# A second wave's input projection moved between the first wave's expert lists, in buffers of its own

## The chip, the cores and the metric

The kernel runs on one NeuronCore of a Trainium2 chip. The metric is the device time of one execution in microseconds; 1798.25 us is the median of three runs before the change (1796.3 to 1800.18).

## The reference

One decoder layer works on 512 prompt tokens and 8 sample tokens, all in f32, model width 1024.

```
x_n   = rmsnorm(x) * g1
proj  = x_n @ w_in                # 3584 columns: attention q,k,v; retention q,k,v; gate
cat   = [dilated attention (8 heads x 64) | gated retention (4 heads x 128)]
h     = x + cat @ w_out
hn    = rmsnorm(h) * g2
q     = hn @ w_pq                 # 8 heads x 2 x 128
top16 of q @ sub_keys, twice; 256 sums of pairs -> top16: 16 expert ids and weights g per head
a     = gelu(sum(u[eid] * hn))    # 8 x 16 experts of 16384, each one row of 1024
y     = h + sum(g * a * v[eid])
out   = rmsnorm(y) * gf
```

The samples attend to a cache of 2048 keys and carry a retention state. Keys, values and states are outputs too.

## The kernel before, in words

The 512 prompt tokens go through in two waves of 256. The 8 samples ride with the first wave up to the end of their mixer, and with the second from its output projection on.

The experts are handled in two ways. The first wave's 256 tokens and the samples *gather*: for each of their 16 experts per head GpSimd issues an indirect DMA that brings one row of `peer_u` to each of 128 partitions (line 907, 128 x 1024 f32), VectorE takes the dot product with the token (line 925), and later does the same with `peer_v` and a weighted sum (line 939). One such fetch with its VectorE work is a *step*: 512 of them for the first wave, 32 for the samples (on 64 partitions). Eight buffers hold rows. The second wave's 256 tokens are *dense*: for each of 128 blocks of 128 experts, `dense_a` multiplies all tokens by a block of `peer_u` (`ut`, line 1054), `dense_w` multiplies by a mask of weights (line 1169), `dense_y` by a block of `peer_v` (`vt`, line 1176). The masks come from `scatter` (lines 1142 to 1157), a chunk of 64 blocks at a time.

In the order of the program: the first wave's input projection, attention and retention, with the samples' attention; its output projection and norm (`outer(0)`, which leaves `hn` in `hnD`); its lists (`product_keys(0)`: projection `w_pq`, scores `psco`, copied to `sc`, top-16 on VectorE at lines 253 to 353); the second wave's load, norm, input projection `in_proj(1)` in 28 blocks of 128 columns, `outer(1)` and `product_keys(1)`, whose result overwrites `hnD`; the scatter of chunk 0; then the dense loop.

The gather steps are one generator, `work`. `beside` runs some steps of it after every block of another generator, by the table `STEPS`; `run` in the scatter loop takes `SOON` steps over 32 groups, and the dense loop takes `RATE - EARLY - SOON` over 128 blocks, where `EARLY` counts the earlier ones. A scheduler of the framework then settles the order of each engine's queue, within the dependencies. Each engine works its queue strictly in order, and so does SyncE, which issues the loads of weights and the stores.

Pools on the right side of the on-chip memory are stacked: a pool opened after another has closed takes over its bytes, and its first writer waits for the last reader there. Thus `x1B`, `xTB` and `catB` of the second wave lie where the lists of the first wave had their temporaries.

Of the kernel before, what the change touches and what calls it, by code (L numbers as in the profile page):

```python
# [34 lines left out]
GBUFS, UTB, VTB, OHB, AHEAD = 8, 4, 4, 2, 19  # L35
ORDER = "aayyyy"
FIRST = 6
SCB = 4
PTB = 2
FOLD = True  # L40
LASTA = False
CHUNKS = [0, 64, 128]
ROWS = max(b - a for a, b in zip(CHUNKS, CHUNKS[1:]))
NG = DT // 8
STEPS = (8, 3, 2, 6)
SOON, RATE = 48, 600
AHEAD0 = 14


# [1 line left out]
def step_kernel(ctx, tc, x_prompt, x_sample, cache_k, cache_v, state_ret, norm1_g, w_in, ret_gn_g,  # L51
# [20 lines left out]
    ps = front.enter_context(tc.tile_pool(name="ps", bufs=2, space=PSUM))  # L72
    wp = front.enter_context(tc.tile_pool(name="wp", bufs=2, side="right"))
    fc = front.enter_context(tc.tile_pool(name="fc", bufs=1, side="right"))
    smp = ExitStack()
    sp = smp.enter_context(tc.tile_pool(name="sp", bufs=1))
    kvp = smp.enter_context(tc.tile_pool(name="kvp", bufs=2))
# [342 lines left out]
    def attention(w, hp2, q2, put):  # L420

        po = ps_tile("o", "po")
        bh = [wide("bh", "bh") for j in range(2)]
        for j in range(2):
            nc.scalar.activation(bh[j], bias, AF.Copy, scale=SLOPES[2 * hp2 + j])
        for t in range(2):
            T = 2 * w + t
            n = (T + 1) * 128
            off = 384 - 128 * T
            pTs = []  # L430
            for j in range(2):
                psc = ps_tile("s", "psc")
                nc.tensor.matmul(psc[:, :n], q2[j][:, t * 128:(t + 1) * 128], keys[hp2][:, :n], start=True, stop=True)
                lg = wide("lg", "lg", 3)[:, :n]
                nm = small.tile([128, 1], F32, name="nm", tag="nm")
                nc.vector.tensor_tensor_reduce(out=lg, in0=psc[:, :n], in1=bh[j][:, off:off + n],
                                               scale=-0.125, scalar=-LOWEST, op0=OP.add, op1=OP.min, accum_out=nm)
                nc.scalar.activation(lg, lg, AF.Exp, bias=nm, scale=-1.0)
                sm = small.tile([128, 1], F32, name="sm", tag="sm")
                nc.vector.tensor_tensor_reduce(out=lg, in0=lg, in1=mult[:, off:off + n],  # L440
                                               scale=1.0, scalar=0.0, op0=OP.mult, op1=OP.add, accum_out=sm)
                rs = small.tile([128, 1], F32, name="rs", tag="rs")
                nc.vector.reciprocal(rs, sm)
                nc.scalar.activation(lg, lg, AF.Copy, scale=rs)
                pT = ps_tile("tr", "pT")
                for s in range(T + 1):
                    nc.tensor.transpose(pT[:, s * 128:(s + 1) * 128], lg[:, s * 128:(s + 1) * 128], ident)
                pTs.append(wide("pTs", "pTs", PTB)[:, :n])
                nc.scalar.activation(pTs[j], pT[:, :n], AF.Copy)
            for s in range(T + 1):  # L450
                for j in range(2):
                    nc.tensor.matmul(po[j * 64:(j + 1) * 64, t * 128:(t + 1) * 128],
                                     vals[hp2][:, s, j * 64:(j + 1) * 64],
                                     pTs[j][:, s * 128:(s + 1) * 128], start=(s == 0), stop=(s == T))
        put(po[:, :WT], hp2)

    def groupnorm(pool, po, p, nb, tag="tr"):
# [5 lines left out]
        for b in range(nb):  # L463
            nc.vector.bn_aggr(mv[:p, b, :], bs[:p, b, :])
        r = rstd_of(mv[:p, :nb, 1], 1.0, 1e-5, p, nb, tag)
        yo = pool.tile([128, 512], F32, name="yo", tag="pTs", bufs=PTB if pool is pools["ap"] else 1)
        for b in range(nb):
            nc.vector.tensor_scalar(yo[:p, b * 128:(b + 1) * 128], po[:p, b * 128:(b + 1) * 128],
                                    mv[:p, b, 0:1], r[:p, b:b + 1], op0=OP.subtract, op1=OP.mult)
# [10 lines left out]
    def retention(w, h, rqT, rkT, kdN, rvN):  # L480
        pin = ps_tile("s", "pin")
        for T in range(2):
            cs = slice(T * 128, (T + 1) * 128)
            nc.tensor.matmul(pin[:, cs], rkT[:, cs], rqT[:, cs], start=True, stop=True)
        inn = wide("lg", "inn", 3)[:, :WT]
        nc.vector.tensor_tensor(out=blk(inn), in0=blk(pin[:, :WT]), in1=dmat[:, h:h + 1, :].to_broadcast([128, 2, 128]),
                                op=OP.mult)
        qd = wide("bh", "qd")[:, :WT]
# [390 lines left out]
    all_of(in_proj(0, xT, [k * 4 + h for h in range(1, 4) for k in range(3, 7)], putA))  # L879
    mixA.close()  # L880

    def outer(w, c2, hn, outs):

        ost = ExitStack()
        op_ = ost.enter_context(tc.tile_pool(name="op", bufs=1, side="right"))
        x = op_.tile([128, 2, D], F32, name="xo")
        xs = op_.tile([8, D], F32, name="xs") if w else None
        load_x(w, x, xs)
        ssq2 = small.tile([128, 3, KB], F32, name="ssq2", tag="ssq2", bufs=1)
        nc.vector.memset(ssq2, 1.0)  # L890
        yield from out_proj(op_, c2, x, xs, ssq2)
        norm2(op_, w, x, xs, ssq2, hn)
        ost.close()
# [54 lines left out]
            w = w2  # L948
        return y, x

    def finish(halves, p, x, dst):

        for q, y in enumerate(halves):
            cs = slice(q * 512, (q + 1) * 512)
            nc.vector.tensor_tensor(out=x[:p, cs], in0=y, in1=x[:p, cs], op=OP.add)
        o = pe.tile([128, D], F32, name="fin", tag="fin")
        ssq = small.tile([128, 1], F32, name="ssqf", tag="ssqf")
        nc.scalar.activation(o[:p], x[:p], AF.Square, accum_out=ssq[:p])
        r = rstd_of(ssq[:p], D, 1e-6, p)
# [17 lines left out]

    def gathered():
        y, x = yield from experts(lists[0], [hnr[:128, :]], slice(0, 128))
        store = finish((y[:, 0:512], y[:, 512:]), 128, x, yp2[0:128, :])  # L980
        y, x = yield from delayed(experts(lists[1], [hnr[128:GT, :]], slice(128, GT)), 12, store)
        store = finish((y[:, 0:512], y[:, 512:]), 128, x, yp2[128:GT, :])
        y64, x = yield from delayed(experts(listS, [hnr[GT:, :]] * 8, slice(512, 520)), 12, store)
        yS = gp.tile([128, D], F32, name="yS", tag="rows")[:8]
        for q in range(2):
            ph = banks["a"]()
            nc.tensor.matmul(ph[:8], selT, y64[:, q * 512:(q + 1) * 512], start=True, stop=True)
            nc.scalar.activation(yS[:, q * 512:(q + 1) * 512], ph[:8], AF.Copy)
        finish((yS[:, 0:512], yS[:, 512:]), 8, x, y_s.rearrange("b t d -> (b t) d"))()

    work = gathered()

# [18 lines left out]
    def run(g, n=1):  # L1011
        for _ in range(n):
            if g is not None:
                next(g, None)

    hst = ExitStack()
    beside(product_keys(0, lists[:2], None, hnA), 8, 0)
    run(work, STEPS[0])
    mixB = ExitStack()
    cpB = mixB.enter_context(tc.tile_pool(name="cpB", bufs=1, side="right"))  # L1020
    catB = cpB.tile([128, KB, WT + 8], F32, name="catB")
    inB = ExitStack()
    xtB = inB.enter_context(tc.tile_pool(name="xtB", bufs=1, side="right"))
    xTB = xtB.tile([128, KB, WT], F32, name="xTB")
    xst = ExitStack()
    xp = xst.enter_context(tc.tile_pool(name="xpB", bufs=1, side="right"))
    x1 = xp.tile([128, 2, D], F32, name="x1B")
    load_x(1, x1)
    norm1(xp, x1, None, lambda pt, k: nc.scalar.activation(xTB[:, k, :], pt, AF.Copy, scale=g1T[:, k:k + 1]))
    xst.close()  # L1030
    pools["ap"] = inB.enter_context(tc.tile_pool(name="apB", bufs=2, side="right"))

    def putB(bank, cb):
        nc.scalar.activation(catB[:, cb, :WT], bank, AF.Copy)

    nc.vector.tensor_copy(catB[:, :, WT:], catS)
    beside(in_proj(1, (xTB,), [k * 4 + hp for hp in range(4) for k in range(3)] +
                   [k * 4 + h for h in range(4) for k in range(3, 7)], putB), 28, STEPS[1])
    inB.close()
    beside(outer(1, (catB,), hnD, None), 8, STEPS[2])  # L1040
    mixB.close()
# [41 lines left out]
        run(first, 2 * (AHEAD0 * (h + 1) // PH - AHEAD0 * h // PH))  # L1083

    beside(product_keys(1, lists[2:], listS, hnD), 8, STEPS[3], early)
    EARLY = step[0] + STEPS[0]
    front.close()

    den = ExitStack()
# [204 lines left out]
```

## Time and profile before

| | |
|---|---|
| median of three runs | 1798.25 us |
| profiled execution: own time, span | 1801.39, 1799.6 us |
| busy in the span: TensorE, VectorE, ScalarE, GpSimd | 1518.8, 1207.2, 420.1, 798.9 us |
| read from memory, over the span | 495.56 MB, 281 GB/s |

All times of rows are microseconds from the start of the span. A matmul of f32 data leaves two records, so a line that the program holds 256 times stands with x512. DVE is VectorE, PE TensorE, POOL GpSimd, SP SyncE.

### The profile page before, as it was taken

The page shows a single profiled execution, that of the slowest core. Times are in us where ns is not written, and L with a number is a line of the kernel's source. Part 1 is how long each engine was busy: PE and PEld are TensorE (multiplying, and loading weights), DVE is VectorE, ACT ScalarE, POOL GpSimd, SP SyncE. Part 2 cuts the span into 40 slices and gives each one's busy share as a digit, 9 for nine tenths or more (in the row PEclk, how much of TensorE's full clock was granted, in tenths as well). Part 3 has the DMA queues.
Part 4 walks back from the last instruction along what each step waited for, and adds up shares of the span by engine and source line. Part 5 has one row for each costly group of instructions (what it writes and reads, how often), then busy time and mean ns, then how long its engine had stood idle before and what let it go on. Part 6 is the DMA issues. An engine that isn't in the chain of part 4 may idle for free.

```text
span 1799.6 us, 21781 instructions
## 1 busy us (share of the span) xinstructions
PE 1518.8 (84%) x7544; PEld 1113.2 (62%) x7544; DVE 1207.2 (67%) x2893; ACT 420.1 (23%) x849; POOL 798.9 (44%) x672
## 2 busy tenths in 40 slices
PE   5977779105898769995469999999999999999997
PEld 5976547104677558884356666666666666666643
DVE  5776517998688643879997775667665555555573
ACT  6734402103532221324331121111111000000001
POOL 2155220287456550005876554444445445455550
PEclk9988889657999879995569999999999999999999
DMA  7576564499899972436759999999999899999995
GB/s 201 154 216 225 185 205 150 130 347 387 280 354 368 366 275 78 158 113 221 228 191 352 400 408 334 340 347 342 347 347 348 340 367 362 370 356 360 309 243 166
DMA packets 213327, 506.89 MB, mean 282 GB/s; under 512 B 16424, under 2 KB 103000, under 8 KB 213088
## 3 DMA queue, kind: packets, MB, share of 16 engines
q0 software_dynamic: 82208, 295.80, 45.9%
q1 hardware_dynamic: 131008, 209.68, 34.6%
q8 instruction: 60, 0.98, 0.2%
q14 instruction: 51, 0.42, 0.1%
HBM read 495.56 MB, written 9.86 MB: 281 GB/s over the span
## 4 chain that ended last, share of the span: by engine, by line
PE 66%; DVE 14%; DMA 10%; issue 2%; ACT 1%; POOL 1%; SPq 0%; DVEq 0%; ACTq 0%; POOLq 0%
PE y L1176 23%; PE pa L1054 21%; PE pa L152 11%; DVE u L925 3%; PE pg L1155 3%; PE paF L1054 3%; DMA raw<-in_w_in 2%; DVE y L939 2%; DVE oi L1149 1%; DMA vt<-in_peer_v 1%; DMA hs<-xo 1%; DMA raw<-in_w_out 1%; DMA pq<-sq_d 1%; DMA u<-in_peer_u,eidL 1%; DVE oj L1144 1%
## 5 line engine op out<-in xcount | busy, mean ns | idle before, releaser
L907 POOL DMA_INDIRECT u<-in_peer_u,eidL x256 | 337.4, 1318 | 321.6 <-DVE a L925 90.3
L1176 PE MATMUL y<-vt,ge 128*128 128x512 f32 x1024 | 462.4, 598 | 3.6 <-DMA vt<-in_peer_v 3.6
L907 POOL DMA_INDIRECT v<-in_peer_v,eidL x256 | 335.0, 1309 | 273.0 <-DVE y L939 115.6
L1054 PE MATMUL pa<-hnD,ut 128*128 128x256 f32 x1792 | 407.7, 381 | 2.5 <-ACT ge L1058 2.0
L1054 PEld LDWEIGHTS pa<-hnD,ut 128*128 128x128 f32 x1792 | 339.5, 191 | 78.2 <-issue 35.1
L939 DVE SCALAR_TENSOR_TENSOR y<-v,gw,y 128x1024 f32<-128x1024 f32 (+1 forms) x269 | 345.1, 1283 | 32.3 <-DMA v<-in_peer_v,eidL 16.4
L925 DVE CUSTOM_DVE_ANT_0 u<-u,hq 128x1024 f32<-128x1024 f32 (+1 forms) x272 | 324.2, 1221 | 18.3 <-DMA u<-in_peer_u,eidL 14.9
L1176 PEld LDWEIGHTS y<-vt,ge 128*128 128x128 f32 x1024 | 196.4, 192 | 207.0 <-issue 194.8
L1169 DVE TENSOR_TENSOR ge<-ge,big 128x256 f32<-128x256 f32 x128 | 51.2, 427 | 187.8 <-ACT ge L1058 179.2
L1058 ACT ACTIVATE ge<-pa 128x256 f32<-128x256 f32 x112 | 42.6, 381 | 475.3 <-PE pa L1054 472.3
L1155 PEld LDWEIGHTS <-oj 128*128 128x128 bf16 x1536 | 101.2, 167 | 83.2 <-DVE oi L1149 62.8
L152 PE MATMUL pa<-hnD,raw 128*128 128x256 f32 (+1 forms) x512 | 122.6, 393 | 0.0
L152 PE MATMUL pa<-xTB,raw 128*128 128x256 f32 x448 | 107.0, 393 | 10.5 <-DMA raw<-in_w_in 10.0
L152 PEld LDWEIGHTS pa<-hnD,raw 128*128 128x128 f32 x512 | 97.8, 196 | 19.9 <-issue 5.9
L1155 PE MATMUL pg<-oi,oj 128*128 128x64 bf16 x1152 | 77.8, 233 | 33.6 <-DVE oi L1149 33.6
L152 PEld LDWEIGHTS pa<-xTB,raw 128*128 128x128 f32 x448 | 86.3, 198 | 25.4 <-issue 7.0
L1144 DVE TENSOR_TENSOR oj<-iota,l 128x1024 bf16<-128x1024 bf16 x64 | 44.2, 692 | 71.0 <-PE pg L1155 71.0
L1157 ACT ACTIVATE big<-pg 128x512 f32<-128x512 f32 x48 | 52.8, 1099 | 152.7 <-PE pg L1155 150.3
L391 PE MATMUL pt<-ident,x1B 128*128 128x128 f32 x16 | 3.6, 388 | 95.2 <-ACT x1B L386 95.2
L121 PE MATMUL pa<-xT,wh 128*128 128x264 f32 x224 | 70.3, 315 | 9.8 <-ACT xT L114 4.8
L253 DVE MAX8 valL<-sc 128x8 f32<-128x128 f32 x64 | 14.3, 280 | 90.6 <-ACT sc L845 76.8
L122 PE MATMUL pa<-xT,wh 128*128 128x264 f32 x224 | 68.2, 305 | 0.1
(515 smaller groups left out, 1852.4 us busy)
## 6 DMA issues: line engine op xcount, KB each, us to landing
ut<-in_u_turned SPq DMA_DIRECT2D x128, 512.0 KB, 6.7
vt<-in_peer_v SPq DMA_DIRECT2D x128, 512.0 KB, 4.4
raw<-in_w_in SPq DMA_DIRECT2D x56, 512.0 KB, 6.6
raw<-in_w_pq SPq DMA_DIRECT2D x16, 1024.0 KB, 5.2
raw<-in_w_out SPq DMA_DIRECT2D x8, 1024.0 KB, 9.8
kv<-in_cache_k_win POOLq DMA_DIRECT2D x24, 256.0 KB, 5.1
kv<-in_cache_v_win POOLq DMA_DIRECT2D x24, 256.0 KB, 3.9
u<-in_peer_u,eidL POOLq DMA_INDIRECT x256, 7.6
```

Of the source, the lines that this page charges most:

```text
L121: nc.tensor.matmul(out, wh, xh, start=first, stop=False)
L122: nc.tensor.matmul(out, wh, xl, start=False, stop=False)
L152: nc.tensor.matmul(pa[:, :n], part[:, k, :], x[0][:, k, :], start=(k == 0), stop=(k == KB - 1))
L907: nc.gpsimd.indirect_dma_start(out=t[:p], out_offset=None, in_=tab, in_offset=bass.IndirectOffsetOnAxis(ap=d["eid"][:p, h, k:k + 1], axis=0))
L925: nc.vector.tensor_tensor_reduce(out=u[:p], in0=u[:p], in1=hn, scale=1.0, scalar=0.0, op0=OP.mult, op1=OP.add, accum_out=a[:, k:k + 1])
L939: nc.vector.scalar_tensor_tensor(y, v[:p], w[:, k:k + 1], y, op0=OP.mult, op1=OP.add)
L1054: nc.tensor.matmul(pa, ut[:, k, :], hnD[:, k, :DT], start=(k == 0), stop=(k == KB - 1))
L1144: nc.vector.tensor_tensor(out=oj, in0=iota128, in1=lJ[:, None, ts].to_broadcast([128, 128, 8]), op=OP.is_equal)
L1155: nc.tensor.matmul(pg_[:, t * ni:(t + 1) * ni], oj[:, :, t], oi3[:, z, :, es], start=(z == 0), stop=(z == 2))
L1157: nc.scalar.activation(place(c, n), pg_.rearrange("p (t i) -> p t i", i=ni), AF.Copy)
L1169: last_ = nc.vector.tensor_tensor(out=gs, in0=gs, in1=wt, op=OP.mult)
L1176: nc.tensor.matmul(yps[b][q], ge[:, b * 128:(b + 1) * 128], vt[:, q * 512:(q + 1) * 512], start=(i == 0), stop=(i == NKEY - 1))
```

## The change

It touches five things. The second wave's `catB` and `xTB` get pools that are opened at the program's start, and its load and norm are written before the first wave's output projection, not behind its lists. `in_proj(1)` becomes a generator of which two blocks run after each of the eight heads of `product_keys(0)`; the other 12 follow. The gather steps are dealt out anew: 16 ahead of those 12 blocks, 7 beside each of them, 5 beside each of the eight blocks of the output projection, 3 beside each head of the second lists, 24 in the first scatter, and a total rate of 590. To make room, `sc` has three buffers, the attention's `lg` and `pTs` are narrower in the first wave, `yo` has buffers of its own, and `finish` writes its result into the buffer of `y` in place of `fin`.

```diff
-SCB = 4
+SCB = 3
-STEPS = (8, 3, 2, 6)
-SOON, RATE = 48, 600
+STEPS = (16, 7, 5, 3)
+BLOCKS = 2
+SOON, RATE = 24, 590
...
+    mixB = ExitStack()
+    cpB = mixB.enter_context(tc.tile_pool(name="cpB", bufs=1, side="right"))
+    inB = ExitStack()
+    xtB = inB.enter_context(tc.tile_pool(name="xtB", bufs=1, side="right"))
...
-                lg = wide("lg", "lg", 3)[:, :n]
+                lg = wide("lg", "lg", 3, 256 + 256 * w)[:, :n]
...
-                pTs.append(wide("pTs", "pTs", PTB)[:, :n])
+                pTs.append(wide("pTs", "pTs", PTB, 256 + 256 * w)[:, :n])
...
-        yo = pool.tile([128, 512], F32, name="yo", tag="pTs", bufs=PTB if pool is pools["ap"] else 1)
+        yo = pool.tile([128, nb * 128], F32, name="yo", tag="yo", bufs=2 if pool is pools["ap"] else 1)
...
     mixA.close()
 
+    catB = cpB.tile([128, KB, WT + 8], F32, name="catB")
+    xTB = xtB.tile([128, KB, WT], F32, name="xTB")
+    xst = ExitStack()
+    xp = xst.enter_context(tc.tile_pool(name="xpB", bufs=1, side="right"))
+    x1 = xp.tile([128, 2, D], F32, name="x1B")
+    load_x(1, x1)
+    norm1(xp, x1, None, lambda pt, k: nc.scalar.activation(xTB[:, k, :], pt, AF.Copy, scale=g1T[:, k:k + 1]))
+    xst.close()
...
-    def finish(halves, p, x, dst):
+    def finish(halves, o, p, x, dst):
...
-        o = pe.tile([128, D], F32, name="fin", tag="fin")
...
-        store = finish((y[:, 0:512], y[:, 512:]), 128, x, yp2[0:128, :])
+        store = finish((y[:, 0:512], y[:, 512:]), y, 128, x, yp2[0:128, :])
...
-    hst = ExitStack()
-    beside(product_keys(0, lists[:2], None, hnA), 8, 0)
-    run(work, STEPS[0])
...
-    load_x(1, x1)
-    norm1(xp, x1, None, lambda pt, k: nc.scalar.activation(xTB[:, k, :], pt, AF.Copy, scale=g1T[:, k:k + 1]))
...
-    beside(in_proj(1, (xTB,), [k * 4 + hp for hp in range(4) for k in range(3)] +
-                   [k * 4 + h for h in range(4) for k in range(3, 7)], putB), 28, STEPS[1])
+    second = in_proj(1, (xTB,), [k * 4 + hp for hp in range(4) for k in range(3)] +
+                     [k * 4 + h for h in range(4) for k in range(3, 7)], putB)
+    for _ in product_keys(0, lists[:2], None, hnA):
+        run(second, BLOCKS)
+    nc.vector.tensor_copy(catB[:, :, WT:], catS)
+    step[0] += STEPS[0]
+    run(work, STEPS[0])
+    beside(second, 28, STEPS[1])
...
-    EARLY = step[0] + STEPS[0]
+    EARLY = step[0]
```

What this does to the queues is seen at three places; the changed kernel's lines are some 4 or 5 higher from line 81 on. On TensorE, at the end of the first wave's lists before, and in their middle now (`hnD,raw` is the projection `w_pq`, `xTB,raw` the second wave's input projection, `psc`, `pT`, `po` its attention):

```order
L841 MATMUL psco<-keysT,qT 128x128 x3
L152 MATMUL pa<-hnD,raw 128x256 x8
L841 MATMUL psco<-keysT,qT 128x128 x4
L391 MATMUL pt<-ident,x1B 128x128 x8
L152 MATMUL pa<-xTB,raw 128x256 x2
L391 MATMUL pt<-ident,x1B 128x128 x4
```

```order
L846 MATMUL psco<-keysT,qT 128x128
L157 MATMUL pa<-xTB,raw 128x256 x8
L438 MATMUL psc<-keys_183,qz_196 128x384
L846 MATMUL psco<-keysT,qT 128x128 x3
L157 MATMUL pa<-xTB,raw 128x256 x2
L482 MATMUL py<-ident,yo 128x8 x4
```

The second wave's projection stood behind the last score product of the lists and behind the transposes of its own input. Now it stands between the score products, and the transposes are far ahead.

On VectorE, at the first top-16 of the second lists (`valL`, `idxL`, `rest`; the line with `u,a<-u,hq` is a gather step), before and now:

```order
L802 TENSOR_SCALAR hnD<-pt_5093,gT 128x256
L802 TENSOR_SCALAR hnD<-pt_5100,gT 128x256
L253 MAX valL_5129<-sc 128x8 x2
L253 MAX valL_5131<-sc 128x8 x2
L255 MAX_INDEX idxL_5130<-valL_5129,sc 128x8
L257 MATCH_REPLACE rest<-valL_5129,sc 128x128
```

```order
L264 MAX valL_5229<-rest 128x8 x2
L940 ISA u,a<-u,hq 128x1024
L940 ISA a 128x1
L264 MAX valL_5231<-rest 128x8 x2
L266 MAX_INDEX idxL_5230<-valL_5229,rest 128x8 x2
L266 MAX_INDEX idxL_5232<-valL_5231,rest 128x8 x2
```

Before, no gather step stood among the second lists; now 53 do.

On TensorE at the end (`y<-vt,ge` is the dense output product, one block is four of them; `selT` sums the samples' gathered result over their heads), before and now:

```order
L987 MATMUL pa_6279<-y,selT 8x512
L987 MATMUL pa_6278<-y,selT 8x512
L1176 MATMUL y_6282<-vt,ge 128x512
L1176 MATMUL y_6283<-vt,ge 128x512
L1176 MATMUL y_6284<-vt,ge 128x512
L1176 MATMUL y_6285<-vt,ge 128x512
```

```order
L1001 MATMUL pa_6306<-y,selT 8x512
L1001 MATMUL pa_6305<-y,selT 8x512
L1180 MATMUL y_6309<-vt,ge 128x512
L1180 MATMUL y_6310<-vt,ge 128x512
L1180 MATMUL y_6311<-vt,ge 128x512
L1180 MATMUL y_6312<-vt,ge 128x512
L1294 UNCONDITIONAL_BRANCH
```

Before, 24 output products (six blocks) stood behind the two with `selT`; now four (one block) and the end of the program.

## Rows read from the trace of the kernel before

**Rows 1.** Stretches: start:end, us, busy us (instructions) per engine, clock, DMA share, GB/s.
```profile
263.20:349.00 85.80, 58.48 (x281) 46.35 (x279) 71.19 (x470) 18.25 (x37) 3.08 (x4) 0.87 0.41 127
349.00:420.00 71.00, 0.00 (x0) 0.00 (x0) 64.79 (x125) 5.36 (x9) 56.48 (x48) 0.50 0.97 354
420.00:623.00 203.00, 177.28 (x871) 141.52 (x872) 155.62 (x314) 73.51 (x147) 120.02 (x96) 0.95 0.99 346
623.00:662.00 39.00, 20.21 (x87) 15.54 (x86) 27.15 (x52) 13.11 (x49) 24.57 (x18) 0.72 0.95 348
662.00:813.00 151.00, 148.48 (x725) 129.95 (x724) 87.79 (x550) 35.85 (x74) 0.00 (x0) 0.99 0.36 116
813.00:939.00 126.00, 63.70 (x811) 54.62 (x810) 124.16 (x201) 51.17 (x78) 91.27 (x47) 0.54 0.67 214
939.00:1709.00 770.00, 770.00 (x3266) 525.49 (x3265) 477.48 (x673) 90.87 (x178) 389.92 (x312) 1.00 0.96 354
1709.00:1799.60 90.60, 77.93 (x173) 32.69 (x171) 51.88 (x80) 11.42 (x22) 25.38 (x24) 0.93 0.75 204
```

**Rows 2.** Waits from 250 to 430: waiter <- releaser: total us, times, longest.
```profile
PE pt L391 <- ACT x1B L386: 95.2, 1, 95.2
POOL u L907 <- DVE posu L261: 81.1, 1, 81.1
```

**Rows 3.** Stretches, line 925 on VectorE alone: busy us (records), clock, DMA, GB/s.
```profile
349.00:662.00 313.00, 109.78 (x182) 0.82 0.98 348
813.00:939.00 126.00, 25.32 (x42) 0.54 0.67 214
```

**Rows 4.** The same for line 939 on VectorE.
```profile
349.00:662.00 313.00, 80.68 (x63) 0.82 0.98 348
813.00:939.00 126.00, 32.26 (x25) 0.54 0.67 214
```

**Rows 5.** Matmul groups of the span by form: xcount | busy us, mean ns | idle.
```profile
L152 PE MATMUL pa<-hnD,raw 128*128 128x256 f32 x256 | 61.8, 392 | 0.0
L152 PE MATMUL pa<-xTB,raw 128*128 128x256 f32 x448 | 107.0, 393 | 10.5 <-DMA raw<-in_w_in 10.0 <-ACT qz L538 0.4
L841 PE MATMUL psco<-keysT,qT 128*128 128x128 f32 x128 | 22.2, 291 | 12.4 <-ACT qT L831 12.4
L391 PE MATMUL pt<-ident,x1B 128*128 128x128 f32 x16 | 3.6, 388 | 95.2 <-ACT x1B L386 95.2
```

**Rows 6.** The second wave's attention on TensorE, 250 to 820, by line.
```profile
L433 PE MATMUL psc<-keys,qz 128*128 128x384 f32 (+1 forms) x32 | 14.1, 544 | 0.0
L447 PE MATMUL pT<-ident,lg 128*128 128x128 f32 x56 | 9.1, 280 | 0.0
L452 PE MATMUL po<-pTs,vals 128*64 128x128 f32 x112 | 10.9, 283 | 0.0
```

**Rows 7.** DMA issues of the page: xcount, KB each, median us to landing.
```profile
ut<-in_u_turned SPq DMA_DIRECT2D x128, 512.0 KB, 6.7
raw<-in_w_in SPq DMA_DIRECT2D x56, 512.0 KB, 6.6
raw<-in_w_out SPq DMA_DIRECT2D x8, 1024.0 KB, 9.8
```

**Rows 8.** Lines 253 and 802: ns min/median/max, first and last start us, forms.
```profile
L253 DVE MAX8 valL<-sc x64: 270/277/296, 263.2 to 776.6; 128x8 f32<-128x128 f32 x64
L802 DVE TENSOR_SCALAR hnD<-pt,gT x8: 483/484/484, 228.5 to 661.2; 128x256 f32<-128x256 f32 x8
```

**Rows 9.** Waits from 1709 to 1770, the sums of the samples.
```profile
DVE y L939 <- DMA v<-in_peer_v,eidS: 11.9, 14, 1.7
```

**Rows 10.** Timeline near the end: start us, us, engine, line, operation.
```profile
1711.14 1.21 DVE L925 CUSTOM_DVE_ANT_0 u<-u,hq 64x1024 f32<-64x1024 f32 x1
...
1764.45 1.28 DVE L939 SCALAR_TENSOR_TENSOR y<-v,gw,y 64x1024 f32<-64x1024 f32 x1 [0.50 <-DMA v<-in_peer_v,eidS]
1767.90 1.88 PE L987 MATMUL pa<-y,selT 64*8 64x512 f32 x4
```

More of the change, by code (lines that the diff above doesn't have):

```diff
@@ L484, in retention @@
             nc.tensor.matmul(pin[:, cs], rkT[:, cs], rqT[:, cs], start=True, stop=True)
-        inn = wide("lg", "inn", 3)[:, :WT]
+        inn = wide("lg", "inn", 3, 256 + 256 * w)[:, :WT]
         nc.vector.tensor_tensor(out=blk(inn), in0=blk(pin[:, :WT]), in1=dmat[:, h:h + 1, :].to_broadcast([128, 2, 128]),
@@ L979, in gathered @@
         y, x = yield from experts(lists[0], [hnr[:128, :]], slice(0, 128))
-        store = finish((y[:, 0:512], y[:, 512:]), 128, x, yp2[0:128, :])
+        store = finish((y[:, 0:512], y[:, 512:]), y, 128, x, yp2[0:128, :])
         y, x = yield from delayed(experts(lists[1], [hnr[128:GT, :]], slice(128, GT)), 12, store)
-        store = finish((y[:, 0:512], y[:, 512:]), 128, x, yp2[128:GT, :])
+        store = finish((y[:, 0:512], y[:, 512:]), y, 128, x, yp2[128:GT, :])
         y64, x = yield from delayed(experts(listS, [hnr[GT:, :]] * 8, slice(512, 520)), 12, store)
@@ L988, in gathered @@
             nc.scalar.activation(yS[:, q * 512:(q + 1) * 512], ph[:8], AF.Copy)
-        finish((yS[:, 0:512], yS[:, 512:]), 8, x, y_s.rearrange("b t d -> (b t) d"))()
+        finish((yS[:, 0:512], yS[:, 512:]), y64, 8, x, y_s.rearrange("b t d -> (b t) d"))()
     work = gathered()
@@ L1014, in run @@
                 next(g, None)
-    hst = ExitStack()
-    beside(product_keys(0, lists[:2], None, hnA), 8, 0)
-    run(work, STEPS[0])
[L1019 to L1027, printed above, removed]
-    load_x(1, x1)
-    norm1(xp, x1, None, lambda pt, k: nc.scalar.activation(xTB[:, k, :], pt, AF.Copy, scale=g1T[:, k:k + 1]))
-    xst.close()
     pools["ap"] = inB.enter_context(tc.tile_pool(name="apB", bufs=2, side="right"))
```

## The prediction

> **What bounds the kernel now.** I read the table of stretches first, since the whole-span shares mix stages with different limits [rows 1]. It shows five stages behind 263 us. The reader should see in it: from 263 to 349 the lists of the first wave, with VectorE at 71.2 of 85.8 us; from 349 to 420 no matmul at all, while VectorE is at 64.8 of 71 and the DMA engines at 0.97; from 420 to 662 the second wave's two projections, with the DMA engines at 0.99 and 0.95; from 662 to 813 the second lists, TensorE at 148.5 of 151, not one gather on GpSimd (its busy time is 0.00) and DMA at 0.36; from 813 to 939 the first scatter, where VectorE is at 124.2 of 126 and TensorE at half clock. From 939 to 1709 TensorE is busy in every microsecond, so whatever is won before 939 arrives at the end, if nothing new appears in that stage or in the last 90.6 us. Second, the waits [rows 2]: the gap around 349 to 420 is one wait of 95.2 us, of the first transpose of the second wave for its normalised rows, and GpSimd itself stood 81.1 us until the first list existed. Third, the gathers by line [rows 3, 4]: on VectorE 91 dot products cost 109.78 us and 63 sums 80.68 us up to 662, so 154 cost 190.5, or 1.24 us each. The kernel therefore has a stage of saturated DMA (349 to 662) next to a stage with DMA nearly unused (662 to 813), and a hole in TensorE ahead of both.
>
> **The change part by part.** I count instructions in the rebuilt orders and take durations from rows. Up to the last row of the second wave's `hnD` (661.2 us now, [rows 8]) VectorE had 155 gathers and now has 110; among the second lists it had none and now has 53; in the first scatter it had 46 [rows 3, 4] and now has 24. So 187 stand before the dense stage in place of 201.
>
> *Start.* The second wave's load and norm move ahead of the first wave's output projection. On TensorE that is 16 transposes, 3.6 us [rows 5], and the `xo` loads on SyncE now stand behind them, because their buffer is the one that `x1B` leaves. What queues behind `xo` there is `g2b`, one weight block of the output projection and the first of `w_pq`. It costs between -5 us (nothing, and the sample attention's matmuls stand earlier) and +8; I take 0. The first list operation stays at 263.2 [rows 8].
>
> *Lists beside projection.* From there to the end of the fourth attention, TensorE's new order holds 96 matmuls of `w_pq` (a record pair each: 192 x 61.8/256 = 46.3 us), 112 of the second wave (224 x 107.0/448 = 53.5), 27 of the 64 score products (22.2 x 27/64 = 9.4) [rows 5], all attention (14.1 + 9.1 + 10.9) [rows 6] and some 8 us of small transposes: 151 us. VectorE's share of this stretch (lists, attention, 16 gathers) is about 100 us and lies beside it. Between 420 and 623 the same mix left TensorE idle for 26 of 203 us [rows 1], 13%; between 662 and 813, 2%. I take 6%: 160 us, with 151 to 171 as the ends. That point is at 423 us.
>
> *Rest of the projection, output projection, norm.* VectorE's busy time up to `hnD` was 71.2 + 64.8 + 155.6 + 27.2 = 318.8 [rows 1]. Without 45 gathers (55.8) and the 100 already done, 163 are left. DMA: 94 gathers of 512 KB (as large as a `ut` tile), 13 blocks of `w_in`, 4 of `w_out` [rows 7] and 4.5 MB of the rest are 65 MB; at 346 to 354 GB/s [rows 1] 184 to 188 us. Ends: 163 (VectorE alone) and 163 x 313/247.6 = 206 (the same stretch's present ratio of time to VectorE work). I take 190, the nearest row being the DMA rate. `hnD` is ready at 613, 49 us earlier than 662.
>
> *Second lists.* TensorE's work is unchanged, 148.5 us. VectorE's 87.8 [rows 1] grow by 53 x 1.24 to 153.5, and DMA to 17.5 + 27.8 = 45 MB or 130 us. Both engines now need about 150 us and are tied through three score buffers (four before). Ends 151 and 153.5 x 1.264 = 194; I take 170. The stage ends at 783.
>
> *First scatter.* 22 gathers fewer at 1.25 us [rows 3, 4] take 27.5 from 126 us, since VectorE is the engine that is full there: 98.5 (97 to 101). The dense stage starts at 881.5, 57.5 us earlier than 939.
>
> *Dense stage.* TensorE's 770 us stay. The gathers per block go from 396/128 to 402/128, hidden as now under DMA 0.96. Without that cover the 14 gathers moved here would cost about 14 x 0.52 MB / 354 GB/s = 21 us; I take 0.
>
> *Tail.* Behind the last multiplication of `ge`, VectorE now has 10 full `v` gathers and the 32 of the samples instead of 32. The 32 ran from 1711 to 1765.7 [rows 10], 1.7 us each. The product with `selT` stands behind 20 of the last 21 output blocks where it stood behind 15. On TensorE's queue only one block waits behind it, and that block's result ends the kernel. Also `finish` now writes its result into `y`, so on SyncE the store `out<-y` stands ahead of ten `vt` loads and waits for VectorE; TensorE waits for those. Ten gathers at 1.3 to 3.4 us are 13 to 34 us, of which TensorE's own 21 blocks hide some 10 to 20. I take +10, ends 0 and +25.
>
> Buffers without `fin`, the smaller `lg`, `pTs` and `yo` cost nothing: `yo` no longer shares with `pTs`, and the row store it now shares with `y` falls some twenty gathers before the next write of `y`, beside which it lands.
>
> Sum against the profiled execution (span 1799.6, its own time 1801.39): 1801.4 - 57.5 + 10 = 1754. The median of the runs shown, 1798.25, lies 3.1 lower, so **1751 us**.
>
> **A rule weighed.** TensorE's granted clock was 0.95 from 420 to 623, where it was 87% busy, 0.72 from 623 to 662 at 52%, and 0.54 in the scatter at 51% [rows 1]. In my second step TensorE has some 120 us of work in 190 (of the 177.3 + 20.2 from 420 to 662, 53.5 and 34.1 are done before, and the last `w_pq` matmuls come to it), so it may lose its level of 2.4 GHz. At 0.72 it needs 167 us, still hidden; at 0.54 it needs 222, or 32 us more. The Trainium skill, "TensorE: Matmul & The Clock Gate", section "HAM oscillation — how this bites in real kernels", says that short idle stretches while waiting for DMA keep putting the clock down; by that rule the second case holds, and the trace agrees for the scatter and not for 420 to 623.
>
> **The rivals.** (1) Slower: the gathers put between lists and attention hold up what stands behind them in VectorE's in-order queue. Place: the two steps from 423 to 783. In the last stretch 14 sums waited 11.9 us for their rows [rows 9], 0.85 each. At that price 94 gathers make the first step 163 + 80 = 243 and 53 make the second 153.5 + 45 = 198.5, or 81 us more: 1832. It decides from 0.62 us per gather (the two steps then take 47.5 us more). For it: three score buffers instead of four, DMA at 0.97 and more. Against it: from 349 to 420 with DMA at 0.97, VectorE still worked 64.8 of 71 us.
> (2) The hole comes back nearly whole: both engines meet their lower ends, 151, 163 and 151: 55 us better, 1696. For it: 53 gathers go where DMA was at 0.36. Against it: VectorE and TensorE would wait for each other nowhere.
> (3) The idle time only moves: VectorE stays at its present share of 263 to 939, 530.8/675.8 = 78.5%. Then 14 gathers fewer (17.5 us) give 653.8 us, 22 won, 10 lost in the tail: 1786. For it: the fetching, which fills the hole at 349 now, starts only behind three attentions.
> (4) The clock falls as above: 1783. For it: the two stretches at 52% and 51%. Against it: 420 to 623.
>
> **Chances.** Forecast 0.62, with its own range 1720 to 1782; (1) 0.10, (2) 0.09, (3) 0.13, (4) 0.06. A measurement of this kernel tells about 0.2% (3.6 us) from no change. Faster then holds the forecast, (2), (4) and half of (3), 0.83; within 0.2% the worse end of (3), 0.06; slower (1) and the worst of the forecast, 0.11. The range takes in (3) and (4) and stops short of (1) and (2): 1716 to 1793.
>
> **What would show it.** Right: no TensorE wait above 20 us between 263 and 420; the last row of `hnD` near 613; GpSimd busy among the second lists; the scatter below 105 us; TensorE unbroken from about 882. Wrong: sums of the second lists waiting 0.6 us or more for rows; TensorE waiting for score buffers; a granted clock near 0.5 in the second wave's projection; `selT` or the last `vt` loads late by more than 25 us; gaps in the dense stage.

## The result and the profile after

The changed kernel takes 1725.01 us in the median of four executions (1721.56 to 1735.22), the kernel before 1797.34 beside it: a ratio of 0.9605, with a 95% interval of 0.9561 to 0.9648, 71 us. The forecast was 1751 within 1716 to 1793. The profiled execution of the changed kernel is the slowest of its four (1735.22, span 1733.3), 66.3 us shorter in span than that of before (1799.6).

The table of stretches of the changed kernel, cut at the same events as [rows 1] (columns as there; 423 is the end of the second wave's fourth attention):

```profile
0.00:270.80 270.80, 206.41 (x1365) 168.54 (x1366) 149.10 (x440) 128.20 (x273) 90.78 (x126) 0.92 0.64 190
270.80:349.00 78.20, 78.20 (x412) 62.74 (x411) 47.21 (x276) 30.65 (x63) 0.00 (x0) 1.00 0.48 143
349.00:423.00 74.00, 62.31 (x323) 49.99 (x322) 60.73 (x214) 25.00 (x50) 38.48 (x31) 0.91 0.86 297
423.00:605.70 182.70, 113.60 (x486) 91.97 (x485) 155.78 (x388) 41.01 (x109) 112.95 (x88) 0.79 0.96 340
605.70:762.00 156.30, 145.11 (x686) 124.78 (x685) 149.82 (x637) 35.54 (x75) 65.66 (x55) 0.96 0.82 290
762.00:857.00 95.00, 61.97 (x831) 57.55 (x830) 93.95 (x155) 48.69 (x74) 48.65 (x26) 0.60 0.56 179
857.00:1640.00 783.00, 783.00 (x3292) 529.87 (x3293) 491.71 (x702) 94.11 (x183) 396.48 (x317) 1.00 0.95 353
1640.00:1733.30 93.30, 74.75 (x161) 29.83 (x159) 60.87 (x86) 10.82 (x21) 33.66 (x33) 0.93 0.86 225
```

The stretch without a matmul (called the hole below) has gone: TensorE is busy for all of 270.8 to 349 and for 62.3 of the next 74 us. GpSimd, at zero among the second lists before, now works there for 65.7 us, with VectorE at 149.8 of 156.3. The first scatter is shorter, the dense stage as full as before.

The lines that mark the steps, in the changed kernel (as in rows 8: least, median and largest duration, first and last start): first and last read of a score list, the four lists of expert ids, the second wave's `hnD`, the scatter's first compare, the dense output products.

```profile
L258 DVE MAX8 valL<-sc x64: 261/276/296, 270.8 to 711.7; 128x8 f32<-128x128 f32 x64
...
L351 DVE SCALAR_TENSOR_TENSOR eidL<-pick,pick x4: 207/214/224, 364.0 to 499.1; 128x64 int32<-128x64 f32 x4
...
L807 DVE TENSOR_SCALAR hnD<-pt,gT x8: 469/483/485, 239.7 to 605.7; 128x256 f32<-128x256 f32 x8
...
L1149 DVE TENSOR_TENSOR oi<-iotaE,lx x64: 406/417/471, 766.8 to 1270.1; 128x512 bf16<-128x512 bf16 x64
...
L1180 PE MATMUL y<-vt,ge x1024: 592/592/1202, 856.7 to 1721.0; 128*128 128x512 f32 x171
```

The last two of these lines in the kernel before:

```profile
L1145 DVE TENSOR_TENSOR oi<-iotaE,lx x64: 412/422/452, 817.7 to 1344.1; 128x512 bf16<-128x512 bf16 x64
...
L1176 PE MATMUL y<-vt,ge x1024: 592/593/1199, 930.5 to 1790.0; 128*128 128x512 f32 x171
```

Against [rows 8] the last row of `hnD` starts at 605.7 in place of 661.2. The first compare of the scatter stands at 766.8 in place of 817.7, the first dense output product at 856.7 in place of 930.5, the end of the span at 1733.3 in place of 1799.6. So up to `hnD` the change wins 55.5 us; from there to the scatter it loses 4.6 (161.1 for 156.5); in the scatter it wins 22.9 (89.9 for 112.8); behind it, it loses 7.5 (876.6 for 869.1). That is 66.3.

TensorE's waits in the changed kernel from 263 to 420, the longest (columns as in rows 2), and its largest sum of the whole span:

```profile
PE pa L157 <- DMA raw<-in_w_pq: 7.2, 1, 7.2
...
PE py L482 <- DVE yo L479: 36.6, 5, 13.0
```

Where one wait of 95.2 us stood [rows 2], the longest is now 7.2. What has grown is the wait at line 482, 3.9 us in all in the kernel before: the retention's transposes wait for `yo`, four times in the second wave, up to 13.0 us, with gather steps between the small operations that lead to `yo` in VectorE's queue.

What made the hole is read from SyncE's longest wait between 200 and 450 in the kernel before, and from the dot products (line 925, two records each) that VectorE ran from the first list of ids to the last one:

```profile
SPq L168 <- DVE eidL L346: 79.1, 1, 79.1
```

```profile
343.30:400.50 57.20, 38.83 (x64) 0.50 0.89 319
```

The load of `x1B` waited 79.1 us for the last operation on the lists' temporaries, whose bytes it takes over. And that operation stood at 400.5, 57.2 us behind the first list, since 32 gather steps with 38.8 us of VectorE's time lay between. So the gathers lengthened the hole; how long it would be if they were held back until the lists are done, no run tells.

### The profile page after: what moved, and what is told of

It reads as the page before. It is cut to its first block, busy times and chain, and to the rows that moved or that the text cites. A ratio compares the mean times of both kernels' runs of the same rounds, so it can differ in the third digit from the quotient of the medians.

```text
span 1733.3 us, 21787 instructions
## 1 busy us (share of the span) xinstructions
PE 1525.3 (88%) x7544; PEld 1115.3 (64%) x7544; DVE 1209.2 (70%) x2893; ACT 414.0 (24%) x846; POOL 786.7 (45%) x672
## 4 chain that ended last, share of the span: by engine, by line
PE 65%; DVE 17%; DMA 10%; issue 4%; ACT 1%; POOL 1%; SPq 0%; DVEq 0%; POOLq 0%; ACTq 0%
PE y L1180 23%; PE pa L1058 22%; PE pa L157 8%; DVE u L940 3%; DVE y L954 3%; DMA vt<-in_peer_v 3%; PE pg L1159 3%; DVE oi L1153 2%; DMA raw<-in_w_out 2%; PE paF L1058 1%; DMA raw<-in_w_pq 1%; DVE oj L1148 1%; DMA pq<-sq_d 1%; PE psc L438 1%; PE pa L127 1%
## 5 line engine op out<-in xcount | busy, mean ns | idle before, releaser
L922 POOL DMA_INDIRECT v<-in_peer_v,eidL x256 | 322.3, 1259 | 317.9 <-DVE y L954 125.0
L1159 PE MATMUL pg<-oi,oj 128*128 128x64 bf16 x1152 | 76.8, 231 | 15.0 <-DVE oi L1153 14.4
L128 PE MATMUL pa<-xT,wl 128*128 128x264 f32 x224 | 67.7, 302 | 0.6 <-DVE wl L120 0.6
L1153 DVE TENSOR_TENSOR oi<-oi,lx 128x1536 bf16<-128x1536 bf16 x64 | 60.4, 949 | 0.0
```

The source lines that it names most:

```text
L128: nc.tensor.matmul(out, wl, xh, start=False, stop=last)
L922: nc.gpsimd.indirect_dma_start(out=t[:p], out_offset=None, in_=tab, in_offset=bass.IndirectOffsetOnAxis(ap=d["eid"][:p, h, k:k + 1], axis=0))
L1153: marks[c] = nc.vector.tensor_tensor(out=oi3, in0=oi[:, None].to_broadcast([128, 3, ne, 64]), in1=lx[:, 1:, None].to_broadcast([128, 3, ne ...
L1159: nc.tensor.matmul(pg_[:, t * ni:(t + 1) * ni], oj[:, :, t], oi3[:, z, :, es], start=(z == 0), stop=(z == 2))
```

## The experiments

Two explanations stand against each other. Theory A: the second wave's input is ready early, and that is enough; the gathers that no longer fit ahead of `hnD` then lie among the second lists, where they cost almost nothing. Theory B: the gain is the projection work written between the first lists, under VectorE's top-16. Counts of gathers are those of VectorE's written order; by time the traces show up to two more in a scatter. The table that says how many gather steps stand where is called the deal. All ratios are to the kernel before on the same chip.

**The buffers and the early norm alone.**

```diff
-STEPS = (16, 7, 5, 3)
-BLOCKS = 2
-SOON, RATE = 24, 590
+STEPS = (8, 3, 2, 6)
+BLOCKS = 0
+SOON, RATE = 48, 600
```

> The changed kernel with the deal of gathers from before (8, 3, 2, 6; 48 in the scatter; rate 600) and no projection block between the first lists; only the buffers, the early norm and the smaller temporaries are left of the change. Theory A (what pays is that the second wave's input is ready and that gathers lie among the second lists, where they cost next to nothing): rows of hnD end within 12 us of the 605.7 of the changed kernel, the scatter is 20 to 27 us longer than its 94.7, time 1735 to 1752. Theory B (what pays is projection work written between the first lists, under VectorE's top-16): TensorE is left with 58 of 86 us in the lists again, hnD comes 25 us later or more, time 1765 to 1785.

Measured: 1725.12 us, 0.9596 (0.9557 to 0.9635), the same as the whole change and 10 us below the range that theory A gave. `hnD`, the first compare and the first dense product of this run, and its stretch from the first id list to `hnD`:

```profile
L807 DVE TENSOR_SCALAR hnD<-pt,gT x8: 469/484/485, 242.5 to 593.4; 128x256 f32<-128x256 f32 x8
...
L1149 DVE TENSOR_TENSOR oi<-iotaE,lx x64: 412/422/451, 743.4 to 1273.0; 128x512 bf16<-128x512 bf16 x64
...
L1180 PE MATMUL y<-vt,ge x1024: 592/592/1200, 858.4 to 1718.5; 128*128 128x512 f32 x171
```

```profile
347.90:593.40 245.50, 178.94 (x866) 141.19 (x865) 203.41 (x485) 79.97 (x183) 155.40 (x121) 0.86 0.99 352
```

`hnD` is not later but 12.3 us earlier than in the changed kernel; the scatter is 115.0 us, 25.1 longer, as 44 gathers stand in it. Theory B has no gain left to explain: there is no block between the lists. With the old deal VectorE's order holds 113 gathers ahead of `hnD` and 42 among the second lists, where the kernel before had 155 and none: how many stand ahead followed the time that there was, and not the table.

**No blocks between the first lists, the new deal.**

```diff
-STEPS = (16, 7, 5, 3)
-BLOCKS = 2
+STEPS = (16, 3, 5, 3)
+BLOCKS = 0
```

> The changed kernel with no projection block between the first lists; all 28 blocks follow with 3 gathers each (84, as the 12 blocks with 7 have now), the rest of the new deal as it is. Theory A: 1712 to 1733, because the first list is ready some 13 us earlier and the gathers start earlier by as much. Theory B: 1745 to 1770, since 53 us of TensorE's work return to the time after the lists.

Measured: 1709.28 us, 0.9511 (0.947 to 0.9552); in six executions on another chip (told further below), 1714.35, 0.9545 (0.951 to 0.958). This is below the changed kernel, whose interval (0.9561 to 0.9648) the first of these does not touch and the second just does, and it is the fastest version found; the first is also below the range that theory A gave. It differs from the run ahead of it by the deal alone, so the new deal is worth 15.8 us on this chip (1725.12 to 1709.28): the scatter is 25.3 us shorter (89.7 for 115.0), and part of that is given back behind it and in the second lists. The two blocks between the lists, put back, take as much away again. The rows of this run and the stretches between them:

```profile
L351 DVE SCALAR_TENSOR_TENSOR eidL<-pick,pick x4: 212/262/309, 345.6 to 423.7; 128x64 int32<-128x64 f32 x4
...
L807 DVE TENSOR_SCALAR hnD<-pt,gT x8: 469/484/485, 240.8 to 589.2; 128x256 f32<-128x256 f32 x8
...
L1149 DVE TENSOR_TENSOR oi<-iotaE,lx x64: 412/421/484, 744.1 to 1248.1; 128x512 bf16<-128x512 bf16 x64
...
L1180 PE MATMUL y<-vt,ge x1024: 592/592/1201, 833.8 to 1696.6; 128*128 128x512 f32 x171
```

```profile
345.60:589.20 243.60, 178.77 (x861) 140.90 (x861) 203.39 (x485) 80.07 (x183) 154.09 (x121) 0.87 1.01 355
589.20:744.10 154.90, 146.65 (x706) 126.42 (x704) 150.46 (x650) 37.04 (x83) 70.08 (x53) 0.99 0.80 286
```

The first id list is at 345.6 in place of 364.0. No gather can start before it. From it to `hnD` 243.6 us pass here, 245.5 with the old deal and 241.7 in the changed kernel, each time at 343 to 355 GB/s. The blocks between the lists do not shorten that stretch beyond the 5 us by which it differs between two executions of the same kernel (243.6 and, in the later one, 248.7); they delay its start.

**The norm back behind the first lists**, all else as in the run without blocks:

```diff
-    load_x(1, x1)
-    norm1(xp, x1, None, lambda pt, k: nc.scalar.activation(xTB[:, k, :], pt, AF.Copy, scale=g1T[:, k:k + 1]))
...
     all_of(product_keys(0, lists[:2], None, hnA))
+    load_x(1, x1)
+    norm1(xp, x1, None, lambda pt, k: nc.scalar.activation(xTB[:, k, :], pt, AF.Copy, scale=g1T[:, k:k + 1]))
```

> The run without blocks between the first lists (1709.28), with one thing undone: the second wave's load and norm stand behind the first lists again, as in the kernel before; the buffers of catB and xTB stay their own. VectorE's order then has 155 gathers ahead of hnD and 8 among the second lists, as the deal of gathers is the same but there is time for them. Theory A (the load of x1B waits for the first lists' temporaries, and this wait alone makes the hole): a TensorE wait of 80 us or more comes back, hnD ends 305 to 320 us after the first list as in the kernel before, time 1765 to 1795. Rival: the buffers of catB and xTB matter too, and half of the gain stays: 1735 to 1760.

Measured: 1775.46 us, 0.9895 (0.9854 to 0.9935). TensorE's longest wait, SyncE's longest between 200 and 450, and the stretch from the first id list to `hnD`:

```profile
PE pt L396 <- ACT x1B L391: 100.8, 1, 100.8
```

```profile
SPq L173 <- DVE eidL L351: 83.6, 1, 83.6
```

```profile
341.80:654.80 313.00, 193.32 (x957) 154.18 (x958) 253.31 (x544) 93.53 (x207) 192.10 (x160) 0.81 0.98 348
```

The hole is back, with the same wait of the load for the lists, and with it 155 gathers ahead of `hnD`. Own buffers for `catB` and `xTB` without an early norm keep little. The time is 20 us under the kernel before (1795.43 beside it), the profiled span 25.1 under it: the scatter with 24 gathers is 23.3 us shorter (89.5 us, first compare 809.2 to first dense product 898.7, for 112.8), the end gives 6.7 of that back (875.8 for 869.1), and `hnD` comes 6.4 us earlier (654.8). Moving these lines forward is worth 0.9895 against 0.9511 and 0.9545, 3.5 to 3.8% or 63 to 69 us. Theory A holds. The hole and the 42 gathers came back together, so this run does not part what each costs; the late norm with those gathers tied behind `hnD` was not run.

**The norm a little later, ahead of the lists but behind the output projection.**

```diff
-    load_x(1, x1)
-    norm1(xp, x1, None, lambda pt, k: nc.scalar.activation(xTB[:, k, :], pt, AF.Copy, scale=g1T[:, k:k + 1]))
...
     all_of(outer(0, catA, hnA, None))
+    load_x(1, x1)
+    norm1(xp, x1, None, lambda pt, k: nc.scalar.activation(xTB[:, k, :], pt, AF.Copy, scale=g1T[:, k:k + 1]))
```

> The run without blocks between the first lists (1709.28), with the second wave's load and norm behind the first wave's output projection and norm, still ahead of its lists. Theory: the 5 to 8 us by which the first list is later than in the kernel before come from the x1B work and from the xo load that waits for its buffer; they go, first operation of the lists at 263 to 268, time 1699 to 1706. Rival: xTB is then ready only in the middle of the lists, and the projection that TensorE does there now (17 us) goes behind them: 1709 to 1725.

Measured: 1715.52 us, 0.9595 (0.9546 to 0.9644). The time lies in the rival's range. The first list operation stood at 273.1, so the expected 263 to 268 was missed; `hnD` ended at 579.3, 9.9 earlier, and the second lists, with 55 gathers, took 159.8 us. Set beside the plain run on one chip:

> The run without blocks between the first lists once more, on the same chip as the next three, so that they can be set against each other: 1706 to 1716.

> The same with the second wave's load and norm behind the first wave's output projection, once more. Its first look gave 1715.52 where the plain one had 1709.28, although its hnD ended 10 us earlier. If the earlier hnD counts it is 3 to 10 us below the run beside it; if it is eaten by the longer stretch of the second lists (55 gathers there in place of 50), the two are within 3 us.

Measured: 1714.35 and 1713.04, 0.9545 (0.951 to 0.958) and 0.9546 (0.9512 to 0.9579): no difference. `hnD` is 10.6 us earlier (581.5 for 592.1), the second lists 6.0 longer (161.2 for 155.2), the rest 2.2 longer.

Why the first list operation did not come earlier is seen on TensorE in the first of the two runs with the later norm (some lines left out; `pav` is the samples' attention):

```profile
247.27 1.05 PE L707 MATMUL pav<-kv,pTz 128*32 128x512 f32 x2 [2.60 <-DMA kv<-in_cache_v_win]
252.11 3.95 PE L707 MATMUL pav<-kv,pTz 128*32 128x512 f32 x8 [3.79 <-DMA kv<-in_cache_v_win]
259.39 3.02 PE L707 MATMUL pav<-kv,pTz 128*32 128x512 f32 x6 [3.33 <-DMA kv<-in_cache_v_win]
262.42 1.06 PE L396 MATMUL pt<-ident,x1B 128*128 128x128 f32 x8
...
267.82 0.49 PE L846 MATMUL psco<-keysT,qT 128*128 128x128 f32 x2 [1.16 <-ACT qT L836]
```

The first transposes for `hnD` start at 224.9, as with the norm behind the lists (225.0; 235.2 in the plain run). But the transposes of `x1B` now stand ahead of the first score product, and ahead of them products of the samples' attention that wait 2.6, 3.8 and 3.3 us for cached values. With the norm behind the lists the first score product starts at 253.5 and the lists at 263.7.

**One block between the lists.**

```diff
-STEPS = (16, 7, 5, 3)
-BLOCKS = 2
+STEPS = (20, 4, 5, 3)
+BLOCKS = 1
```

> The changed kernel with one projection block after each head of the first lists in place of two, and the same number of gathers (164) ahead of the scatter. Theory: what the blocks cost is the delay of the first complete list, from which the gathers and the saturated stretch of 242 us up to hnD start; it is at 345.6 without blocks and at 364.0 with two, so at 351 to 358 with one, hnD 238 to 246 us behind it, time 1713 to 1721. Rival: the cost is in how the gathers are dealt (7 beside each of 12 blocks, ahead of the retention's norm in VectorE's queue); then hnD does not follow the first list by the same 242 us.

Measured: 1728.68 us, 0.9655 (0.9611 to 0.9699), outside the expectation. The list and `hnD`:

```profile
L351 DVE SCALAR_TENSOR_TENSOR eidL<-pick,pick x4: 224/248/260, 354.8 to 462.9; 128x64 int32<-128x64 f32 x4
...
L807 DVE TENSOR_SCALAR hnD<-pt,gT x8: 469/483/484, 238.5 to 592.1; 128x256 f32<-128x256 f32 x8
...
L1149 DVE TENSOR_TENSOR oi<-iotaE,lx x64: 412/421/480, 758.3 to 1261.0; 128x512 bf16<-128x512 bf16 x64
```

```profile
592.10:758.30 166.20, 152.29 (x718) 130.54 (x716) 162.75 (x660) 36.13 (x83) 71.24 (x63) 0.96 0.85 305
```

The first part came out nearly as expected: first list at 354.8, `hnD` 237.3 us behind it. What the expectation lacked is the next stretch, 166.2 us. It holds 60 gathers, and VectorE is at 162.75 of it. So this version pays twice: with a later list, and with a fuller VectorE in the second lists. One block is not measurably better than two (0.9605, 0.9561 to 0.9648).

**No gathers among the second lists.**

```diff
-STEPS = (16, 3, 5, 3)
+STEPS = (16, 2, 4, 0)
```

> The run without blocks between the first lists (1709.28), with 104 in place of 164 gathers dealt out ahead of the scatter: 103 stand ahead of hnD, none among the second lists (50 there), 104 behind the last multiplication of ge (42). It asks what the 50 gathers cost among the second lists, read from hnD to the first oi, 154.9 us now. Theory A: TensorE's 147 us bound that stretch, so it shrinks by 3 to 9 us only, 0.06 to 0.18 us per gather, and the 62 gathers cost far more behind the dense stage: time 1740 to 1790. Rival (VectorE waits for rows at 0.62 us or more per gather among the lists, or VectorE's 1.24 us count in full): the stretch shrinks by 25 us or more.

Measured: 1794.86 us, 0.9999 (0.9973 to 1.0025). The second lists' stretch, VectorE's longest wait in it, and TensorE's longest of the span:

```profile
585.60:742.70 157.10, 150.05 (x727) 130.48 (x726) 92.03 (x566) 37.47 (x82) 0.26 (x2) 0.99 0.37 120
```

```profile
DVE valL L258 <- ACT sc L850: 61.2, 6, 14.1
...
PE pa L1001 <- DVE y L954: 94.2, 1, 94.2
```

Without gathers the stretch takes 157.1 us, with 50 of them 154.9. VectorE, at 92.0 us of work, waits 61.2 for scores that TensorE (150.0) brings; the gathers go into that wait. So the stretch did not even shrink by the 3 to 9 us that theory A expected. At the other end 62 more gathers behind the last `ge` cost 88 us (963.5 from the first dense product to the end, for 875.1), 1.4 each; TensorE's longest wait, 94.2 us, stands there, of the `selT` product for the last sum.

**The gathers ahead of `hnD` fewer.** The steps written among the second lists are tied behind the last `hnD` write:

```diff
-STEPS = (16, 3, 5, 3)
+STEPS = (16, 2, 1, 6)
...
+            if more is not None:
+                with tc.issue_after(hnmark[0].ins):
+                    run(work, per)
+            else:
+                run(work, per)
```

> The run without blocks between the first lists, with 79 in place of 113 gathers ahead of hnD: the deal is 16, 2 per block, 1 per block of the output projection and 6 per head of the second lists, and those of the second lists may not be ordered ahead of hnD. Among the second lists stand 48 (50), in the scatter 24 (24), behind the last multiplication of ge 77 (42). Theory: from the first list to hnD the DMA engines set the time, 0.52 MB at some 354 GB/s or 1.48 us per gather; 34 fewer make the 243.6 us into 190 to 200, hnD ends at 535 to 546. Behind the dense stage the 35 more cost about 1.4 each as 62 did, so the whole time is 1700 to 1722. Rival: that stretch is set by TensorE's and VectorE's chain (179 and 203 us of work, waits for the retention's norm); then hnD ends at 560 to 589 and the time is 1730 to 1765.

Measured: 1737.59 us, 0.969 (0.9647 to 0.9733), the time inside the rival's range, `hnD` at 557.2: between the two expectations, so both had part of it. Two pieces of the stretch that starts at 340.8:

```profile
450.00:500.00 50.00, 37.53 (x177) 30.84 (x178) 40.77 (x93) 11.32 (x23) 30.73 (x26) 0.91 1.00 357
500.00:560.00 60.00, 40.01 (x178) 31.58 (x178) 25.79 (x58) 18.76 (x68) 14.69 (x12) 0.82 0.63 214
```

Until 500 the DMA engines are full as before. Then the 79 gathers are used up, the DMA share falls to 0.63, and the rest of the attention, the output projection and the norm take their time without DMA being full. The stretch took 216.4 us, for 243.6 and 248.7 in the two plain executions: 34 fewer gathers gave 27 to 32 us, 0.8 to 0.95 each; the 1.48 of the expectation does not hold once the gathers are used up. The 35 that moved to the end cost 52.6 us there (927.7 for 875.1), 1.5 each.

**The scatter and the end.** The changed kernel with 48, the kernel before with 24, and the run without blocks with 12:

```diff
-SOON, RATE = 24, 590
+SOON, RATE = 48, 590
```

> The changed kernel with 48 in place of 24 gathers in the first scatter; 45 stand there in VectorE's order in place of 24, and 14 in place of 42 behind the last multiplication of ge. By the term of the prediction (1.25 us for each gather in the scatter) its 94.7 us become 121; the end behind the dense stage becomes 5 to 15 us shorter; time 1733 to 1747. Rival: the scatter waits for its own chain and not for VectorE, and 21 gathers lie beside it for nothing: time 1710 to 1722.

```diff
-SOON, RATE = 48, 600
+SOON, RATE = 24, 600
```

> The kernel before with 24 in place of 48 gathers in the first scatter, nothing else. By the term of the prediction 20 gathers fewer shorten the scatter by 25 us, and 16 more behind the last multiplication give 5 to 15 back: 1780 to 1790. Rival: the gain is given back whole in the dense stage, 1795 to 1799.

```diff
-SOON, RATE = 24, 590
+SOON, RATE = 12, 590
```

> The run without blocks between the first lists, with 12 in place of 24 gathers in the first scatter and 54 in place of 42 behind the last multiplication of ge. By the measured 1.1 us for each gather in the scatter (23 us for 21) it wins 13 there; behind the dense stage 12 more cost 0.4 to 1.4 each, 5 to 17. Theory: nothing is left to win between the two places, 1701 to 1714, within 6 us of the plain run beside it. Rival: the end absorbs them as it absorbed 14 to 42, and it is 8 us or more faster.

Measured: 1736.89 (0.9668, 0.9619 to 0.9716); 1789.77 (0.9949, 0.9921 to 0.9976); 1721.97 (0.9596, 0.9559 to 0.9633). First compare and first dense product of the first two:

```profile
L1149 DVE TENSOR_TENSOR oi<-iotaE,lx x64: 414/422/443, 756.2 to 1282.0; 128x512 bf16<-128x512 bf16 x64
...
L1180 PE MATMUL y<-vt,ge x1024: 592/592/1199, 869.2 to 1725.2; 128*128 128x512 f32 x171
```

```profile
L1145 DVE TENSOR_TENSOR oi<-iotaE,lx x64: 411/422/478, 815.7 to 1319.8; 128x512 bf16<-128x512 bf16 x64
...
L1176 PE MATMUL y<-vt,ge x1024: 592/592/1202, 905.3 to 1766.1; 128*128 128x512 f32 x171
```

From compare to product it is 113.0 us with 45 gathers in the changed kernel, for 89.9 with 24, and 89.6 with 24 in the kernel before, for 112.8: 1.1 us per gather, as forecast in kind (1.25). With 12 it is 79.3 (740.3 to 819.6). The rest of the span, from the first dense product on, is 865.7 us with 14 gathers behind the last `ge`, 869.1 with 32, 876.6 with 42, 885.2 with 48, 892.4 with 54. So the end absorbs some thirty, and past 42 it charges more than a gather's VectorE time (1.24 us): 1.4 to 1.5 each, by the runs without blocks with 42, 54, 77 and 104. Twelve fewer in the scatter gained nothing: 1721.97 beside 1714.35 for the plain run, outside the 6 us that were expected, though the two intervals (0.9559 to 0.9633 and 0.951 to 0.958) still touch.

## Why the prediction was right

The direction and the place were right: the hole closed, `hnD` came earlier by about what was forecast, gathers moved among the second lists, and the first dense product came 73.8 us earlier for a forecast of 57.5. What made the gain was in part another thing than the prediction's second step says, as told below. Step by step, in the profiled executions:

| step | forecast | measured |
|---|---|---|
| start of the first lists | 263.2 | 270.8 |
| end of the fourth attention | 423 | 423 |
| `hnD` ready | 613 | 605.7 |
| from `hnD` to the scatter, change | +19 | +4.6 |
| scatter, change | -27.5 | -22.9 |
| behind it, change | +10 | +7.5 |

The sum was -47.5 and came out as -66.3. Of the 18.8 us missing, 14.4 are the term of the second lists, 6.5 lie ahead of `hnD`, 2.5 at the end, and the scatter gave 4.6 less.

*The mis-sized term* is "Second lists": 170 us chosen between 151 and 194, on the ground that both engines need about 150 and are tied by the score buffers. The pairing cost little. Runs with 0, 8, 42 and 50 gathers there take 157.1, 154.4, 150.0 and 154.9 us; with 53, 55 and 60 they take 161.1, 159.8 and 166.2. That fits TensorE's work (137 to 152 us) as the bound up to some 50 gathers and VectorE's beyond (92.0 + 60 x 1.24 = 166.4). One run lies off it: with the gathers tied behind `hnD`, 48 of them, the stretch took 159.2 us with TensorE at 150.1 and VectorE at 148.1 of it; why, stays open.

*Start:* the 0 was too good; +7.6 is at the bad end of its range. With the norm behind the lists the start is 263.7 again, so the delay comes with the early norm and not with the smaller buffers. Moved behind the output projection, the norm stood in front of the first score product instead, so the start of the lists did not move.

*Lists beside projection:* 423 was met through a late start and a shorter stretch (152.2 for 160). Its value was misjudged all the same. The step treats the blocks between the lists as part of the gain; they gave none and cost some 11 to 17 us (0.9605 with two, for 0.9511 and 0.9545 without). What the prediction had in its third rival, that the fetching starts later, is the cost: 18.4 us at the first id list. That the new deal won about what the blocks lost, so that the whole change comes out at what its buffers and early norm give alone, was not forecast; that the sum lies near its forecast is in so far luck.

*To `hnD`:* DMA as the bound gave the right size, 182.7 us for 190. From the first id list 155 gathers took 317.9 us in the kernel before at 344 GB/s, 110 take 241.7 at 343, 113 take 243.6 at 355. DMA is not the only bound there: with 34 gathers fewer the stretch shrank by 27 to 32 us and not by 50 (34 x 1.48).

*Rivals.* (1) would have needed 0.62 us of waiting per gather. Between 423 and 760 VectorE waited for rows 6.1 us in all:

```profile
DVE u L940 <- DMA u<-in_peer_u,eidL: 6.1, 8, 1.6
```

Its queue did hold `yo` back, 36.6 us of TensorE's waiting, but TensorE had 113.6 us of work in 182.7, with DMA at 0.96. (2), at 1696, came near once the blocks were out: 1709 and 1714. (3) VectorE's share from the first list to the dense stage rose from 78.5% to 507.5 of 586.2 us, 87%. (4) the granted clock did fall, to 0.79 from 423 to 605.7 and 0.70 from 500 to 560, between the levels of 1.2 and 2.4 GHz; the step still took 182.7 us for a forecast of 190, so no price of it is seen. The Trainium skill, "TensorE: Matmul & The Clock Gate", section "HAM oscillation — how this bites in real kernels", says that short idle stretches at DMA waits put the clock down. This trace agrees that the clock fell among short idle stretches, but only 14.5 us of TensorE's waiting there ended with a load and 34.9 with `yo` on VectorE. In the scatter of the kernel before, which the prediction counts for that rule, TensorE's waits ended with VectorE's compares (33.6 and 28.7 us), not with loads.

## What to carry to other kernels

Before writing work in between other work, look for the one load that waits for somebody else's buffer: two pools opened at the start and a norm written earlier (with the smaller temporaries that make room) were worth all 71 us; of the rest, the new deal won some 15 us and the blocks written between the lists cost as much. Where a stretch with full DMA stands beside one in which VectorE waits for TensorE, let the gathers run over into the second; here they were free there up to its idle time, 50 gathers in 61 us of VectorE's waiting. Work put ahead of the first result that releases the DMA stretch delays all of it.

## What had not been expected

A table that deals out steps did not decide where they run: 113 gathers stood ahead of `hnD` whether 108 or 140 were written there, and 155 with the same 140 where the norm stood behind the lists; the time there was, the total and an explicit tie moved them. A gather behind the last `ge` costs between next to nothing (865.7 to 869.1 for 18 more) and 1.5 us (35 more for 52.6); all of them stand ahead of the `selT` products, and these ahead of the end. The same kernel took 1709.28 and 1714.35 us in two sets of runs on two chips (1707.2 to 1712.7 and 1705.42 to 1717.11), and its stretch from the first id list to `hnD` 243.6 and 248.7. That sets the limit of what is told here: differences under some 6 us, of times or of one stretch, are not told apart. The prediction's 0.2% (3.6 us) was too fine; the interval of its own result is 0.9% wide.
